# A hybrid encoder step: squares of the head norm on ScalarE, and the memory's split behind the weight casts

## The chip, the cores and the metric

One core of a Trainium2 chip runs the program: TensorE (PE) multiplies, VectorE (DVE), ScalarE (ACT) and GpSimd (POOL) compute elementwise, SyncE (SP) issues most transfers. The metric is device time of one execution in microseconds. Before the change the median of three runs is 962.3 us (962.19 to 962.57).

## The reference, cut to what matters

The step runs two layers over 256 prompt frames and 32 sample frames (T = 288 columns) with D_MODEL 1024. Layer 0 has one input projection that feeds two groups of heads: A, chunk-band attention, and B, forgetting attention. Both normalise query and key by head (64 rows):

```python
def rmsnorm(x, g):
    xf = x.astype(jnp.float32)
    y = xf * lax.rsqrt(jnp.mean(xf * xf, axis=-1, keepdims=True) + EPS)
    return (y * g.astype(jnp.float32)).astype(x.dtype)
```

Layer 1 has stick-breaking attention without that norm. After its mixer each layer attends across 256 memory tokens, whose keys and values are made from `rmsnorm(mem, g_mem) @ w_kv`, and then runs a squared-ReLU MLP of four times the width. The weights are float32 and are read once; the core reads 148.65 MB in all.

## The kernel before, in words

Activations lie transposed: 128 features on the partitions, 288 frames along the free axis, eight such tiles (`KT`). A product runs as three TensorE products on split operands (`mm3`, lines 156 to 160): high part by high part, high by low, low by high. So each weight is split on the core. `load_chunk` (118 to 145) loads 256 columns of a weight matrix in two halves of 512 KB by SP into a pool of four raw buffers (`wraw`), ACT casts the high part (`wh`, L143, in the first layer's mixer two casts of 128x512 per half), and DVE or POOL subtracts it for the low part (`wl`, L144). Three split halves fit ahead of PE. The activations are split the same way.

`headnorm` (408 to 413) sums squares over 64 partitions by a product with a block-diagonal matrix of ones. The squares too are split in a high and a low part: ACT writes `sqh` (L410), DVE casts it to `sh` (L341) and subtracts to `sl` (L343), both in `two_parts`; PE adds both products up in `ps_hn` (L348, L349); ACT takes logarithm and exponential for the root (L182, L183). It runs 16 times: four projections, query and key, two halves each. `two_parts` also serves the norms of cross attention and of the memory's keys. These tiles and others are drawn from eight scratch buffers of one tag (`f`).

`ORD_AB` (line 32) orders the steps of layer 0's mixer: `q`: query and key of a group, `p`: values, `a`: attention, `F`: the forget gate, `M`: the memory's split (`mem_split`), `N`: the memory's root mean square (`mem_rms`), `K`: the memory's keys of one head. `mem_split` loads the memory in two parts of 512 KB into the same raw buffers as the weights, and in eight steps casts it times a gain (`mh`, ACT L313), subtracts (`ml`, DVE L314), squares (ACT L317, L320) and adds the squares on DVE (L321). `mem_rms` sums over partitions on PE (L332, L335) and takes roots on ACT. In layer 1 the same function runs without the squares and sums.

A planner of the tile framework simulates the whole program with its own costs and writes the order of each engine and of SP's queue; earlier lines have priority, and a buffer is given out as it comes free in that simulation. On the chip each engine then runs its order without change and waits where something is late. `issue_after` puts all instructions of a block behind a given one on that one's engine.

Of the kernel before, what the change touches and what calls it, by code (L numbers as in the profile page):

```python
# [8 lines left out]
F32 = mybir.dt.float32  # L9
F32R = mybir.dt.float32r  # L10
AF = mybir.ActivationFunctionType
ALU = mybir.AluOpType
AX = mybir.AxisListType

P = 128
NP_ = 256
NS = 32
T = NP_ + NS
KT = 8
CW = 256  # L20
FB = 8
# [7 lines left out]
HPE = 0  # L29
HPG = 0  # L30
VT2 = 1
ORD_AB = 'qA0 pA0 F qA1 pA1 aA0 qB0 aA1 qB1 pB0 M pB1 aB0 N K2 aB1 K0 K3 K1'.split()
ORD_C = 'M q0 k0 v0 q1 k1 v1 m0 q2 k2 v2 m1 q3 k3 v3 m2 m3'.split()
FILL_C = 96, 30, 12
ORD_X = 's1 s2 s3 s0 v0 v1 S v2 v3'.split()
# [16 lines left out]
def body(ctx: ExitStack, tc: tile.TileContext, i: dict, o: dict):  # L52
    nc = tc.nc
    mm = nc.tensor.matmul
    dve = nc.vector
    act = nc.scalar.activation

    const = ctx.enter_context(tc.tile_pool(name="const", bufs=1))
    wraw = ctx.enter_context(tc.tile_pool(name="wraw", bufs=WR))
# [4 lines left out]
    scr = ctx.enter_context(tc.tile_pool(name="scr", bufs=2))  # L64
# [7 lines left out]
    class R:  # L72
        stack = None
        count = 0
        step = 4
        c = 0
        after = None
# [18 lines left out]
    def bank(pool, name):  # L96
        return pool.tile([P, 512], F32, tag="b", name=name)
# [20 lines left out]
    def load_chunk(ap, w=CW, split=2, before=None):  # L118

        nk = KT // split  # L120
        ws = []
        for s in range(split):
            raw = wraw.tile([P, nk, w], F32, tag="raw", name="raw")
            if before is None:
                nc.sync.dma_start(out=raw, in_=ap[:, s * nk:(s + 1) * nk, :])
            nq = min(nk, NQ) if split > 1 else nk
            step = min(nq, R.step) if before is None else 1
            for k in range(0, nk, step):
                if k % nq == 0:
                    wh = wspl.tile([P, nq, w], F32R, tag="wh", name="wh")  # L130
                    wl = wspl.tile([P, nq, w], F32R, tag="wl", name="wl")
                    ws += [(wh[:, j, :], wl[:, j, :]) for j in range(nq)]
                r, src = slice(k % nq, k % nq + step), raw[:, k:k + step, :]
                if before is not None:
                    nc.sync.dma_start(out=src, in_=ap[:, s * nk + k:s * nk + k + 1, :])
                    before(s * nk + k)
                R.count += 1
                e = nc.gpsimd if R.pool_every and R.count % R.pool_every == 0 and before is None else dve
                with ahead(HPS):
                    if R.dve_every and R.count % R.dve_every == 0 and before is None:  # L140
                        dve.tensor_copy(wh[:, r, :], src)  # L141
                    else:
                        act(wh[:, r, :], src, AF.Copy)  # L143
                    e.tensor_tensor(wl[:, r, :], src, wh[:, r, :].bitcast(F32), ALU.subtract)  # L144
        return ws

    def ahead(n):
        return tc.high_priority(n) if n else ExitStack()
# [32 lines left out]
    def rstd_of(ps, n, inv, out):  # L181
        act(out, ps, AF.Ln, bias=epsb, scale=inv)  # L182
        act(out, out, AF.Exp, scale=-0.5)  # L183
# [69 lines left out]
    def first(k):  # L253
        nc.scalar.dma_start(out=h[:, k, :], in_=i["xT"][:, k, :])
        n0.split(k)

    ws0 = load_chunk(i["ab_w"][0], before=first)
    xh, xl, rs = n0.rms(SQP)

# [10 lines left out]
    for a in range(4):  # L270
        r = slice(32 * a, 32 * a + 32)
# [11 lines left out]
    bdr = const.tile([P, P], F32R, name="bdr")  # L283
# [13 lines left out]
    memrs = const.tile([P, NP_], F32, name="memrs")  # L297
    memrt = const.tile([P, 2], F32, name="memrt")

    def mem_split(layer, put=None):  # L300

        mh = spp.tile([P, KT, T], F32R, tag="sp", name="mh")
        ml = spp.tile([P, KT, T], F32R, tag="sp", name="ml")
        ssum = scr.tile([P, T], F32, tag="ssum", name="mssum", bufs=2) if layer == 0 else None
        raws = []

        def step(k):
            if k % 4 == 0:
                raws.append(wraw.tile([P, 4, NP_], F32, tag="raw", name="mraw"))
                nc.sync.dma_start(out=raws[-1], in_=i["memT"][:, k:k + 4, :])  # L310
            m = raws[-1][:, k % 4, :]
            g = gT[:, 3, layer, k:k + 1]
            act(mh[:, k, 0:NP_], m, AF.Copy, scale=g)  # L313
            dve.scalar_tensor_tensor(ml[:, k, 0:NP_], m, g, mh[:, k, 0:NP_].bitcast(F32), ALU.mult, ALU.subtract)  # L314
            if layer == 0:
                if k == 0:
                    act(ssum[:, 0:NP_], m, AF.Square)  # L317
                else:
                    sq = scr.tile([P, T], F32, tag="f", bufs=FB, name="sqm")
                    act(sq[:, 0:NP_], m, AF.Square)  # L320
                    dve.tensor_tensor(ssum[:, 0:NP_], ssum[:, 0:NP_], sq[:, 0:NP_], ALU.add)  # L321

        for k in range(KT):
            if put is None:
                step(k)
            else:
                put(k, lambda k=k: step(k))
        return mh, ml, ssum

    def mem_rms(ssum):  # L330
        ps = bank(R.m, "ps_ms")
        mm(ps[:, 0:NP_], ones, ssum[:, 0:NP_], start=True, stop=True)  # L332
        rstd_of(ps[:, 0:NP_], NP_, 1.0 / 1024, memrs)
        for j in range(2):
            mm(ps[:, NP_ + j:NP_ + j + 1], ssum[:, j * P:(j + 1) * P], ones[:, 0:1], start=True, stop=True)  # L335
        rstd_of(ps[:, NP_:NP_ + 2], 2, 1.0 / 1024, memrt)

    def two_parts(sq, n):

        sh = scr.tile([P, T], F32R, tag="f", bufs=FB, name="sh")  # L340
        dve.tensor_copy(sh[:, 0:n], sq[:, 0:n])  # L341
        sl = scr.tile([P, T], F32R, tag="f", bufs=FB, name="sl")
        (nc.gpsimd if HNP else dve).tensor_tensor(sl[:, 0:n], sq[:, 0:n], sh[:, 0:n].bitcast(F32), ALU.subtract)  # L343
        return sh, sl

    def add_parts(ps, sel, parts, n):

        mm(ps[:, 0:n], sel, parts[0][:, 0:n], start=True, stop=False)  # L348
        mm(ps[:, 0:n], sel, parts[1][:, 0:n], start=False, stop=True)  # L349
# [4 lines left out]
    def xnorm_parts(t, n):  # L354
        sq = []
        for d in range(2):
            sq.append(scr.tile([P, T], F32, tag="f", bufs=FB, name="sqx"))
            act(sq[d][:, 0:n], t[:, d, 0:n], AF.Square)
        dve.tensor_tensor(sq[0][:, 0:n], sq[0][:, 0:n], sq[1][:, 0:n], ALU.add)
        return two_parts(sq[0], n)  # L360
# [9 lines left out]
    def mem_k(layer, hd, mh, ml):  # L370
        ws = load_chunk(i["w_kv"][layer, hd])
        t = scr.tile([P, 2, T], F32, tag="t2", name="tmk")
        pss = gemm2(ws, mh, ml, NP_)
        for d in range(2):
            ps = pss[d]
            dve.tensor_tensor(t[:, d, 0:NP_], ps[:, 0:NP_], memrs, ALU.mult)
        return mem_k_norm(layer, hd, t, xnorm_parts(t, NP_))
# [28 lines left out]


    def headnorm(t, r):
        sq = scr.tile([P, T], F32, tag="f", bufs=FB, name="sqh")
        act(sq, t, AF.Square)  # L410
        ps = bank(R.m, "ps_hn")
        add_parts(ps, bdr, two_parts(sq, T), T)
        rstd_of(ps[:, 0:T], T, 1.0 / 64, r)

    def project_qk(wname, cq, ck, xh, xl, rs, norm, ko, oidx, ws0=None):
# [160 lines left out]
    class Mix:  # L576
# [55 lines left out]
        def run(self, steps):  # L632
            xh, xl, rs = self.x
            for step in steps:
                op, g = step[0], int(step[1:] or 0)
                if op == "M":
                    mem = mem_split(1)[0:2]
                elif op == "q":
                    qz = R.ph.tile([P, 2, T], F32, tag="qz", name="qz", bufs=QZB[1])
# [314 lines left out]
    def project_ab(kind, g):  # L954
        return project_qk("ab_w", 6 * kind + g, 6 * kind + 2 + g, xh, xl, rs, kind, "ab"[kind] + "kT", g,
                          ws0 if kind == 0 and g == 0 else None)

    def values_ab(kind, g):
        return project_v("ab_w", 6 * kind + 4 + g, xh, xl, rs, "ab"[kind] + "vT", g)
# [30 lines left out]
    qk, vs, mk0 = {}, {}, {}  # L990
    for step in ORD_AB:
        op, at = step[0], step[1:]
        kind, g = ("AB".index(at[0]), int(at[1])) if len(at) == 2 else (0, 0)
        if op == "q":
            qk[at] = project_ab(kind, g)
        elif op == "p":
            vs[at] = values_ab(kind, g)
        elif op == "a":
            group_ab(kind, g, *qk[at], vs[at])
        elif op == "F":  # L1000
            forget()
        elif op == "M":
            mh, ml, msum = mem_split(0)
        elif op == "N":

            with tc.issue_after(last_mm[0].ins):
                mem_rms(msum)
        else:
            R.after = last_mm[0].ins if at == "0" else R.after
            mk0[int(at)] = mem_k(0, int(at), mh, ml)  # L1010
# [26 lines left out]
    mh, ml = mix.mem  # L1037
# [115 lines left out]
```

## Time and profile before

| what | value |
| --- | --- |
| median of three runs | 962.3 us |
| profiled execution, and its span | 962.2 us, 960.5 us |
| PE, DVE, ACT, POOL busy | 946.5, 686.3, 526.4, 170.9 us |
| mean granted TensorE clock | 0.995 |
| layer 0's mixer | about the first 176 us |
| memory's split | 87.8 to 139.0 us, in pieces |

A page lists busy times by engine, the chain of work that ended last, and groups of instructions by source line, with the idle time of the engine in front of them and what ended it in brackets (`<-`). Timelines give start, duration, engine, line, operation, written tile `<-` read tiles. Matmuls are pipelined, so a matmul that lasts 0.29 us starts every 0.13 us. SPq is SP's queue of transfers.

### The profile page before, as it was taken

Reading aid. Unit: us, or ns where it says so; the run is one execution under the profiler, and the core shown is the slowest. Engines: PE = TensorE matmul, PEld = TensorE weight load, DVE = VectorE, ACT = ScalarE, POOL = GpSimd, SP = SyncE. Lnnn points to the kernel's source line nnn. Section 1 sums busy time; section 2 is a strip of 40 time slices with the busy share of each in tenths; the row PEclk is TensorE's granted clock in tenths of the full one; section 3 lists DMA queues with packets and bytes.
Section 4 is the critical chain, followed back from the end, with each engine's and each line's share of the span. In section 5 each row is a group of like instructions: output and inputs, shape, how many; then the busy total and the mean of one; then the engine's idle time right before and its main releaser. Section 6 shows DMA issues by size and latency. Waiting matters only on the chain.

```text
span 960.5 us, 19226 instructions
## 1 busy us (share of the span) xinstructions
PE 946.5 (99%) x7284; PEld 917.6 (96%) x7284; DVE 686.3 (71%) x1506; ACT 526.4 (55%) x1220; POOL 170.9 (18%) x200
## 2 busy tenths in 40 slices
PE   8998999999999999999999999999999999999998
PEld 7997899999999999999999899999999999999998
DVE  8788788779678766767687567778977655555643
ACT  5666577656456644444466646554644664454531
POOL 4002200021212221222100000003444111111110
PEclk9999899999999999999999999999999999999999
DMA  8654464644555554545465444465444454545452
GB/s 266 220 156 134 134 214 141 232 161 138 172 168 170 160 174 157 175 156 174 156 214 173 151 158 141 142 217 178 139 159 140 152 178 158 172 158 175 155 175 72
DMA packets 50700, 160.01 MB, mean 167 GB/s; under 512 B 6296, under 2 KB 12968, under 8 KB 50352
## 3 DMA queue, kind: packets, MB, share of 16 engines
q1 hardware_dynamic: 46864, 148.69, 48.1%
q0 software_dynamic: 2592, 8.92, 2.4%
q10 hardware_dynamic: 1152, 1.18, 0.4%
q8 instruction: 57, 0.93, 0.4%
q14 instruction: 35, 0.29, 0.1%
HBM read 148.65 MB, written 10.12 MB: 165 GB/s over the span
## 4 chain that ended last, share of the span: by engine, by line
PE 91%; DVE 5%; DMA 1%; issue 1%; ACT 1%; SPq 0%; DVEq 0%
PE g L158 27%; PE g L160 27%; PE g L159 27%; DVE wl L144 2%; DMA mraw<-in_memT_dram 1%; PE zz L753 1%; PE zz L708 1%; PE zz L504 1%; PE s L549 1%; PE sx L158 0%; DVE spl L741 0%; PE sx L160 0%; PE pox L160 0%; DVE ml L314 0%; PE ps_px L822 0%
## 5 line engine op out<-in xcount | busy, mean ns | idle before, releaser
L143 ACT ACTIVATE wh<-raw 128x512 fp32r<-128x512 f32 (+3 forms) x541 | 269.0, 547 | 242.1 <-PE g L159 129.8
L144 DVE TENSOR_TENSOR wl<-raw,wh 128x512 fp32r<-128x512 f32 (+3 forms) x519 | 318.5, 650 | 98.5 <-ACT wh L143 92.4
L158 PE MATMUL g<-xh,wh 128*128 128x288 f32 (+1 forms) x1032 | 305.6, 300 | 1.1 <-DVE t L433 0.5
L159 PE MATMUL g<-xl,wh 128*128 128x288 f32 (+1 forms) x1032 | 304.4, 297 | 1.8 <-DVE xl L196 1.8
L160 PE MATMUL g<-xh,wl 128*128 128x288 f32 (+1 forms) x1032 | 303.4, 298 | 0.6 <-DVE wl L144 0.5
L144 POOL TENSOR_TENSOR wl<-raw,wh 128x256 fp32r<-128x256 f32 (+2 forms) x105 | 123.3, 1174 | 436.6 <-ACT wh L143 328.6
L158 PEld LDWEIGHTS g<-xh,wh 128*128 128x128 f32 (+1 forms) x1032 | 193.3, 189 | 4.1 <-DVE t L433 1.1
L159 PEld LDWEIGHTS g<-xl,wh 128*128 128x128 f32 (+1 forms) x1032 | 193.7, 188 | 3.1 <-DVE xl L196 2.6
L160 PEld LDWEIGHTS g<-xh,wl 128*128 128x128 f32 (+1 forms) x1032 | 193.6, 189 | 2.7 <-DVE wl L144 1.6
L159 PE MATMUL g<-hl,wh 128*128 128x288 f32 x512 | 150.4, 295 | 0.0
L158 PE MATMUL g<-hh,wh 128*128 128x288 f32 x512 | 149.0, 295 | 0.0
L160 PE MATMUL g<-hh,wl 128*128 128x288 f32 x512 | 148.6, 294 | 0.0
L159 PEld LDWEIGHTS g<-hl,wh 128*128 128x128 f32 x512 | 96.1, 188 | 0.0
L160 PEld LDWEIGHTS g<-hh,wl 128*128 128x128 f32 x512 | 95.7, 188 | 0.0
L158 PEld LDWEIGHTS g<-hh,wh 128*128 128x128 f32 x512 | 95.3, 188 | 0.0
L159 PE MATMUL g<-ol,wh 128*128 128x288 f32 x256 | 74.9, 295 | 0.0
L158 PE MATMUL g<-oh,wh 128*128 128x288 f32 x256 | 74.0, 296 | 0.3 <-ACT oh L525 0.3
L160 PE MATMUL g<-oh,wl 128*128 128x288 f32 x256 | 73.5, 295 | 0.0
L141 DVE CAST wh<-raw 128x256 fp32r<-128x256 f32 (+2 forms) x83 | 32.4, 391 | 39.8 <-PE g L159 20.1
L905 DVE TENSOR_TENSOR h<-h,g 128x288 f32<-128x288 f32 x64 | 28.8, 450 | 29.6 <-PE g L160 29.5
L159 PEld LDWEIGHTS g<-ol,wh 128*128 128x128 f32 x256 | 48.1, 188 | 0.0
L158 PEld LDWEIGHTS g<-oh,wh 128*128 128x128 f32 x256 | 47.5, 188 | 0.6 <-ACT oh L525 0.4
(285 smaller groups left out, 1466.4 us busy)
## 6 DMA issues: line engine op xcount, KB each, us to landing
raw<-in_w_up_dram SPq DMA_DIRECT2D x64, 512.0 KB, 3.8
raw<-in_w_down_dram SPq DMA_DIRECT2D x64, 512.0 KB, 3.8
raw<-in_w_kv_dram SPq DMA_DIRECT2D x32, 512.0 KB, 3.8
raw<-in_sb_w_dram SPq DMA_DIRECT2D x24, 512.0 KB, 4.0
raw<-in_ab_w_dram SPq DMA_DIRECT2D x22, 512.0 KB, 4.8
raw<-in_w_q_dram SPq DMA_DIRECT2D x16, 512.0 KB, 3.8
raw<-in_w_o_dram SPq DMA_DIRECT2D x16, 512.0 KB, 3.8
raw<-in_ab_wo_dram SPq DMA_DIRECT2D x8, 512.0 KB, 3.9
```

The lines of the kernel that those rows point to most:

```text
L141: dve.tensor_copy(wh[:, r, :], src)
L143: act(wh[:, r, :], src, AF.Copy)
L144: e.tensor_tensor(wl[:, r, :], src, wh[:, r, :].bitcast(F32), ALU.subtract)
L158: mm(out, lh, rh, start=first, stop=False)
L159: mm(out, lh, rl, start=False, stop=False)
L160: return mm(out, ll, rh, start=False, stop=last)
L504: out.append(mm(po[64 * par:64 * par + 64, kk * P:NP_], vt[:, kk, cols], pts[par][kk], start=kk == 0, stop=kk == 1).ins)
L549: mm(s[:, 0:NP_], q[:, P:NP_], kT[:, p, 0:NP_], start=True, stop=True)
L708: mm(block(zz, e, kk), kT[r, p, kk * P:(kk + 1) * P], qz[r, p, kk * P:NP_].rearrange("p (b c) -> p b c", c=P), start=kk == 0, stop=False, ...
L753: mm(zz[:, e, 0:384], mtrir, x[:, e, :], stop=False, **k_)
L905: dve.tensor_tensor(h[:, kt, :], h[:, kt, :], ps[:, 0:T], ALU.add)
```

## The change

In `headnorm` the first part of the squares is written by a second ACT Square of the same input, with a rounded output, instead of a DVE cast of the first; the subtraction stays on DVE. The other users of `two_parts` keep the cast. `M` moves ahead of `pB0`. In layer 0 the memory's eight steps are only noted there; the two following calls of `load_chunk` (pB0's and pB1's) each issue four of them behind their last ACT cast. Both parts of the memory are now loaded at once, ahead of the steps, in both layers. In `mem_rms` the second sums stand ahead of the first root.

```diff
-ORD_AB = 'qA0 pA0 F qA1 pA1 aA0 qB0 aA1 qB1 pB0 M pB1 aB0 N K2 aB1 K0 K3 K1'.split()
+ORD_AB = 'qA0 pA0 F qA1 pA1 aA0 qB0 aA1 qB1 M pB0 pB1 aB0 N K2 aB1 K0 K3 K1'.split()
...
+        tow = []
...
-                        act(wh[:, r, :], src, AF.Copy)
+                        cast = act(wh[:, r, :], src, AF.Copy).ins
                     e.tensor_tensor(wl[:, r, :], src, wh[:, r, :].bitcast(F32), ALU.subtract)
+        if R.tow:
+
+            now, R.tow = R.tow[0:4], R.tow[4:]
+            with tc.issue_after(cast):
+                for fn in now:
+                    fn()
         return ws
...
-    def mem_split(layer, put=None):
+    def mem_split(layer, tow=False):
...
+        for k in range(0, KT, 4):
+            raws.append(wraw.tile([P, 4, NP_], F32, tag="raw", name="mraw"))
+            nc.sync.dma_start(out=raws[-1], in_=i["memT"][:, k:k + 4, :])
 
         def step(k):
-            if k % 4 == 0:
-                raws.append(wraw.tile([P, 4, NP_], F32, tag="raw", name="mraw"))
-                nc.sync.dma_start(out=raws[-1], in_=i["memT"][:, k:k + 4, :])
-            m = raws[-1][:, k % 4, :]
+            m = raws[k // 4][:, k % 4, :]
...
-        for k in range(KT):
-            if put is None:
-                step(k)
-            else:
-                put(k, lambda k=k: step(k))
+        steps = [lambda k=k: step(k) for k in range(KT)]
+        if tow:
+            R.tow = steps
+        else:
+            for fn in steps:
+                fn()
         return mh, ml, ssum
...
     def mem_rms(ssum):
         ps = bank(R.m, "ps_ms")
         mm(ps[:, 0:NP_], ones, ssum[:, 0:NP_], start=True, stop=True)
-        rstd_of(ps[:, 0:NP_], NP_, 1.0 / 1024, memrs)
         for j in range(2):
             mm(ps[:, NP_ + j:NP_ + j + 1], ssum[:, j * P:(j + 1) * P], ones[:, 0:1], start=True, stop=True)
+        rstd_of(ps[:, 0:NP_], NP_, 1.0 / 1024, memrs)
         rstd_of(ps[:, NP_:NP_ + 2], 2, 1.0 / 1024, memrt)
...
+    def square_parts(t):
+
+        sq = scr.tile([P, T], F32, tag="f", bufs=FB, name="sqh")
+        act(sq, t, AF.Square)
+        sh = scr.tile([P, T], F32R, tag="f", bufs=FB, name="sh")
+        act(sh, t, AF.Square)
+        sl = scr.tile([P, T], F32R, tag="f", bufs=FB, name="sl")
+        dve.tensor_tensor(sl, sq, sh.bitcast(F32), ALU.subtract)
+        return sh, sl
...
     def headnorm(t, r):
-        sq = scr.tile([P, T], F32, tag="f", bufs=FB, name="sqh")
-        act(sq, t, AF.Square)
         ps = bank(R.m, "ps_hn")
-        add_parts(ps, bdr, two_parts(sq, T), T)
+        add_parts(ps, bdr, square_parts(t), T)
         rstd_of(ps[:, 0:T], T, 1.0 / 64, r)
...
-            mh, ml, msum = mem_split(0)
+            mh, ml, msum = mem_split(0, tow=True)
```

## The prediction

> **What bounds the kernel now.** I read the page first, then the time by windows, then the timelines of single engines where a window fell short.
>
> ```profile
> span 960.5 us, 19226 instructions
> ...
> PE 946.5 (99%) x7284; PEld 917.6 (96%) x7284; DVE 686.3 (71%) x1506; ACT 526.4 (55%) x1220; POOL 170.9 (18%) x200
> ...
> PE 91%; DVE 5%; DMA 1%; issue 1%; ACT 1%; SPq 0%; DVEq 0%
> ```
>
> TensorE (PE) is busy 946.5 of 960.5 us, and 91% of the chain that ended last is its own work. The change adds no matmul and removes none, so it can only gain where PE stands idle or runs at a lower clock. The first window below is an undisturbed stretch of the first layer, attention included; the second is the stretch in which the memory's split now runs.
>
> ```profile
> 48.00:76.00 28.00, 28.00 (x210) 26.90 (x209) 21.42 (x71) 18.91 (x52) 1.08 (x2) 1.00 0.54 162
> 76.00:104.00 28.00, 24.92 (x174) 20.52 (x173) 24.58 (x68) 18.23 (x53) 9.48 (x11) 0.88 0.45 144
> 104.00:108.00 4.00, 3.90 (x25) 3.04 (x25) 3.46 (x8) 1.66 (x4) 0.74 (x1) 1.00 0.00 0
> ```
>
> Columns: window, length, busy time and instructions of PE, PE's weight loads, DVE, ACT and POOL, granted clock, DMA share, GB/s. From 76 to 104 PE is idle 3.08 us, and a mean clock of 0.88 costs 0.12 x 28 = 3.4 us more: 6.4 us, with 174 matmuls against 210 in the stretch before. That is nearly all that can be won here. Windows cut at the edges of the clock's steps show where it fell:
>
> ```profile
> 81.24:84.66 3.42, 2.67 (x22) 2.43 (x20) 3.42 (x7) 0.63 (x2) 1.51 (x2) 1.00 0.20 68
> ...
> 91.48:94.90 3.42, 2.10 (x31) 1.46 (x29) 3.38 (x15) 3.42 (x11) 0.32 (x1) 1.00 0.03 9
> 94.90:101.72 6.82, 6.15 (x23) 5.27 (x24) 5.61 (x15) 3.89 (x13) 1.99 (x4) 0.50 0.85 260
> ```
>
> PE idles 1.32 us between 91.48 and 94.90 and the clock is then halved for 6.82 us; 0.75 us of idle time in 81.24 to 84.66 did not do it.
>
> **The first half of the memory's split (a wait that goes).** ACT works in order:
>
> ```profile
> 87.78 0.51 ACT L313 ACTIVATE mh<-mraw,gT 128x256 fp32r<-128x256 f32 x1 [0.97 <-DMA mraw<-in_memT_dram]
> ...
> 88.50 1.29 ACT L313 ACTIVATE mh<-mraw,gT 128x256 fp32r<-128x256 f32 x3
> 89.70 0.49 ACT L491 ACTIVATE pr<-pr,nm 128x256 f32<-128x256 f32 x1
> ...
> 93.15 2.17 ACT L143 ACTIVATE wh<-raw 128x512 fp32r<-128x512 f32 x4
> 95.23 0.29 ACT L533 ACTIVATE qs<-qz 128x128 f32<-128x128 f32 x1
> ```
>
> ```profile
> 91.41 0.29 PE L160 MATMUL g<-xh,wl 128*128 128x288 f32 x1
> 92.11 0.40 PE L348 MATMUL ps_hn<-sh,bdr 128*128 128x288 f32 x1 [0.41 <-DVE sh L341]
> ...
> 95.57 1.11 PE L538 MATMUL ss<-ck,qs 128*64 128x256 f32 x2 [1.58 <-ACT qs L533]
> ```
>
> ACT waits 0.97 us for the memory's transfer and then spends until 89.70 on it: softmax and head norm behind it start 89.70 - (87.78 - 0.97) = 2.9 us late. Afterwards ACT has no gap until qs, and PE stands 1.58 us for qs. With the memory gone from this place, ACT can't be early by all of 2.9 us: the weight casts at 93.15 overwrite buffers that PE reads until 91.70 (91.41 + 0.29). So they move by 93.15 - 91.70 = 1.45, and qs with them. Term 1: -1.45 us (bounds 0 and -1.99, both PE waits).
>
> **The clock.** The 1.45 us brings the idle time of that window from 1.32 to near zero, below the 0.75 that left the clock alone. Term 2: -3.4 us, half of 6.82 (bounds 0 and -3.4). [...]
>
> **The second half.**
>
> ```profile
> 101.45 1.71 ACT L313 ACTIVATE mh<-mraw,gT 128x256 fp32r<-128x256 f32 x4 [2.20 <-DMA mraw<-in_memT_dram]
> ...
> 102.00 3.81 DVE L314 SCALAR_TENSOR_TENSOR ml<-mraw,gT,mh 128x256 fp32r<-128x256 f32 x4 [0.81 <-ACT mh L313]
> ...
> 106.07 0.44 DVE L433 TENSOR_TENSOR t<-g,rs 128x288 f32<-128x288 f32 x1
> ```
>
> ACT waits 2.20 us, then DVE is held 3.81 us by four instructions, and t, which empties a matmul bank, comes at 106.07. PE meanwhile did 25 matmuls in 104 to 108 where an undisturbed 4 us hold 30 (210 over 28 us): 5 x 28/210 = 0.7 us, for the 2.07 us of the hold that lie behind 104. At that rate 3.81 us cost 1.3. Term 3: -1.3 us (bounds 0 and -2.5, a full stop from 104 to the matmul behind t).
>
> **ScalarE writes the first part.** Of 16 head norms each loses a DVE cast and gains a second ACT Square:
>
> ```profile
> L410 ACT ACTIVATE sqh<-t x16: 426/429/444, 21.4 to 123.0; 128x288 f32<-128x288 f32 x16
> L341 DVE CAST sh<-sqh x16: 291/302/1995, 22.4 to 123.6; 128x288 fp32r<-128x288 f32 x16
> ```
>
> In the chain of one norm a cast of 0.30 gives way to a Square of 0.43 that overlaps the one before it (three mh took 1.29, so 0.40 rather than 0.49 each): about +0.04 us, sixteen times +0.6. ACT (65% busy in the quoted 76 to 104) has room, DVE (88%) gains some. Term 4: +0.6 us (bounds -0.5 and +2). [...]
>
> One cast is worth more. POOL's additions on the decay bias hold DVE up:
>
> ```profile
> 79.60 2.09 POOL L975 TENSOR_TENSOR b<-b,cq 128x1024 f32<-128x1024 f32 x1
> ```
>
> ```profile
> 79.86 2.00 DVE L341 CAST sh<-sqh 128x288 fp32r<-128x288 f32 x1
> 84.22 0.44 DVE L343 TENSOR_TENSOR sl<-sqh,sh 128x288 fp32r<-128x288 f32 x1
> ...
> 99.95 1.23 DVE L343 TENSOR_TENSOR sl<-sqh,sh 128x288 fp32r<-128x288 f32 x1
> ```
>
> ```profile
> 84.72 0.40 PE L349 MATMUL ps_hn<-sl,bdr 128*128 128x288 f32 x1 [0.81 <-DVE sl L343]
> ```
>
> The cast begun at 79.86 ends with POOL's addition, and PE later waits 0.81 us for sl. Without the cast, sl takes that place, stretched as at 99.95 to 1.23, so DVE is ahead by 2.00 + 0.44 - 1.23 = 1.2 us, and next in line is the softmax maximum. Term 5: -1.0 us (bounds 0 and -1.6).
>
> **Where the memory's work goes.** Its two loads move ahead of pB0's two on the SP queue:
>
> ```profile
> 77.86 0.37 SPq L125 DMA_DIRECT2D raw<-in_ab_w_dram  x1
> ...
> 96.17 0.35 SPq L310 DMA_DIRECT2D mraw<-in_memT_dram  x1
> ```
>
> ```profile
> DMA to landing us min/median/max: 3.8/3.9/5.3
> ```
>
> All four share the pool of four raw buffers, so pB0's halves take the places in time that the memory had, the second 96.17 instead of 77.86 (no other queue is passed; the steps issue nothing on POOL's). It lands by 96.17 + 5.3 = 101.5, and its cast starts at 108.32 now: 6.8 us of cover, which shrinks as PE gets earlier, though the buffer is then freed earlier too. Term 6: +0.4 us (bounds 0 and +2).
>
> The eight steps now stand behind pB0's and pB1's last casts, about 109 and 120:
>
> ```profile
> 108.32 1.15 ACT L143 ACTIVATE wh<-raw 128x512 fp32r<-128x512 f32 x2 [0.62 <-PE g L159]
> ...
> 127.92 1.94 ACT L320 ACTIVATE sqm<-mraw 128x256 f32<-128x256 f32 x6
> ```
>
> ```profile
> 108.00:118.00 10.00, 9.49 (x88) 8.37 (x87) 6.63 (x16) 5.77 (x13) 0.86 (x2) 1.00 0.46 151
> 118.00:128.00 10.00, 10.00 (x79) 9.98 (x78) 7.30 (x16) 6.38 (x16) 0.54 (x1) 1.00 0.43 149
> ```
>
> Four steps cost ACT 1.71 for the casts and 4 x 0.32 (six squares in 1.94) for squares: 3.0 us. DVE pays four steps at 0.48 and up to four additions at 0.42 (minimum, median, maximum in ns below):
>
> ```profile
> L314 DVE SCALAR_TENSOR_TENSOR ml<-mraw,gT,mh x16: 471/482/1826, 88.3 to 487.5; 128x256 fp32r<-128x256 f32 x16
> ...
> L321 DVE TENSOR_TENSOR mssum<-mssum,sqm x7: 416/419/421, 128.7 to 139.0; 128x256 f32<-128x256 f32 x7
> ```
>
> That is 3.6 us less about four casts saved, 1.2. ACT is idle 4.2 and 3.6 us in the two windows, DVE 3.4 and 2.7: both halves fit, tightly. Queued behind them are the head norms of the last query/key group and pB1's transposed values, on which PE waits. I take half of one block, term 7: +1.5 us (bounds 0 and +6.0, two blocks wholly in PE's way; without the idle time as cover they cost that). The memory's products follow on PE some 4 us behind the second half, so nothing waits for mh:
>
> ```profile
> 127.86 0.28 PE L158 MATMUL g<-mh,wh 128*128 128x256 f32 x1
> ```
>
> **Sums ahead of roots.**
>
> ```profile
> 140.18 0.60 PE L332 MATMUL ps_ms<-mssum,ones 128*128 128x256 f32 x2
> ...
> 141.34 0.61 PE L335 MATMUL ps_ms<-ones,mssum 128*128 128x1 f32 x4
> ```
>
> The second sums wait until ACT's first root has read the bank: 141.34 - 140.78 = 0.56 us, into which PE can put attention work. Nearer to nothing, then. Term 8: -0.2 us (bounds 0 and -0.6).
>
> **Sum.** -1.45 - 3.4 - 1.3 + 0.6 - 1.0 + 0.4 + 1.5 - 0.2 = -4.85. The profiled execution took 962.2 us (span 960.5 and 1.7 around it), 0.1 under the median of 962.3. So 957.4 us.
>
> **The rivals.**
> (A) The half clock stays or moves. The planner orders every engine anew from its own cost model; qs keeps four weight casts in front of it, and a gap of 1 us elsewhere in a thin window does the same. For it: 81.24 to 84.66 already holds 0.75 us of idle time. Against: term 1 closes the one window that fell, and term 5 thins the other. Without term 2: 962.3 - 1.45 = 960.9.
> (B) Slower: the towed blocks. At 109 and 120 ACT and DVE are given 3 us each in one piece; if the planner lets them go ahead of t and r of the last head norms, PE idles up to term 7's bound, and a new gap over 1.32 us in one window halves the clock for 6.8 us. Then +6.0 + 3.4 in place of +1.5: -4.85 + 7.9 = +3.05, 965.3 us. It decides once the new stalls exceed 6.4 us together. For it: DVE would be at 9 of 10 us from 108 on (6.63 + 2.4). Against: PE has weight products to do there, and the blocks wait for no transfer.
> (C) Nothing moves, because the squares can't come early: they need scratch tiles (eight for all norms) which the last head norms hold; the six of 127.92 stand there now though their data was there by 101.45. So the memory's raw buffers stay taken and later loads start late, while the freed time is eaten by the next wait. Terms 1, 3 and 5 halve, the clock term goes, 6 and 7 stay: -1.9 + 2.3 = 962.7.
> (D) More than forecast: blocks and transfers wholly hidden (terms 4, 6, 7 at zero): -7.35, 955.0.
>
> **How the numbers follow.** Forecast 0.42 (own range 955.5 to 960.0), A 0.18, B 0.18, C 0.10, D 0.12. About 0.2%, 1.9 us, is what a measurement tells from no change. Faster: forecast, D, and 0.10 of A, 0.64. Same: 0.08 of A, C's 0.10, 0.18. Slower: B, 0.18. The range 953 to 964.5 takes in D with the clock and other terms near their good bounds, A and C, and B's milder half.
>
> **What would show it.** Step 1: no wait of ACT's mh on the memory's transfer in the first layer, and PE's wait on qs gone or under 0.5 us. Step 2: granted clock 1.00 from 80 to 130. Step 3: no stretched ml beside POOL's additions. Steps 4, 5: no DVE cast under head norm, sh on ACT, ps_hn's wait on sl gone near 84. Step 7: mh behind wh in two groups of four, with PE idle under 1.5 us after each. Wrong it would be if PE showed a new gap behind a towed block, if half clock appeared again, or if wh casts waited on late weights.

## The result, and the profile after

The changed kernel takes 956.46 us (median of four runs, 955.00 to 957.54), the kernel before 962.3 us (962.19 to 962.57). The ratio is 0.9938, with a 95% interval of 0.9921 to 0.9955: 5.8 us faster. Run again later beside other variants it took 954.92 us (five runs, 954.72 to 956.86) against 961.97, a ratio of 0.9933 (0.9921 to 0.9945). The profiled execution of the first set took 956.56 us. Two executions that lie far off the others of their kernel are left out of the medians below: 1296.26 us of the move without the tow, and 3206.80 us of the changed kernel without POOL's additions, the only one of that kernel that was profiled.

The page of the changed kernel: span, busy times, the chain that ended last.

```profile
span 954.8 us, 19232 instructions
...
PE 943.2 (99%) x7284; PEld 917.8 (96%) x7284; DVE 682.9 (72%) x1490; ACT 530.7 (56%) x1236; POOL 171.8 (18%) x200
...
PE 94%; DVE 4%; ACT 1%; issue 1%; DMA 0%; SPq 0%; DVEq 0%; ACTq 0%
```

DVE lost sixteen instructions and ACT gained sixteen, one for each head norm. The same stretches as before, by windows (length, busy time and count of PE, its weight loads, DVE, ACT, POOL, then granted clock, DMA share, GB/s):

```profile
48.00:76.00 28.00, 28.00 (x213) 27.27 (x211) 22.07 (x69) 21.33 (x60) 1.38 (x3) 1.00 0.57 173
76.00:104.00 28.00, 28.00 (x227) 25.09 (x227) 24.23 (x69) 21.10 (x60) 9.97 (x10) 1.00 0.51 161
104.00:108.00 4.00, 2.17 (x17) 1.94 (x16) 4.00 (x8) 1.73 (x5) 1.90 (x2) 1.00 0.39 122
108.00:118.00 10.00, 10.00 (x68) 9.37 (x67) 7.23 (x16) 7.26 (x18) 0.56 (x1) 0.83 0.30 101
```

The bad stretch, 76 to 104, is whole: PE has no idle time, the clock is 1.00, and it does 227 matmuls where it did 174. But a hole that was not there stands at 104 to 108: 2.17 us busy of 4.00, and behind it the clock is halved again (0.50 from 108.22 to 111.63). In the single timelines of PE, DVE and POOL it looks like this (start, duration, engine, line, operation, written tile `<-` read tiles, idle time before):

```profile
107.14 0.40 PE L165 MATMUL g<-xh,wh 128*128 128x288 f32 x1 [1.83 <-DVE vT L481]
```

```profile
97.44 1.29 DVE L145 TENSOR_TENSOR wl<-raw,wh 128x512 fp32r<-128x512 f32 x2 [1.44 <-ACT wh L144]
98.65 1.70 DVE L321 SCALAR_TENSOR_TENSOR ml<-mraw,gT,mh 128x256 fp32r<-128x256 f32 x4
100.91 0.80 DVE L361 TENSOR_TENSOR sl<-sqh,sh 128x288 fp32r<-128x288 f32 x1 [0.57 <-ACT sh L359]
101.64 3.42 DVE L145 TENSOR_TENSOR wl<-raw,wh 128x512 fp32r<-128x512 f32 x2
104.98 0.41 DVE L537 TENSOR_TENSOR ol<-po,oh 128x256 fp32r<-128x256 f32 x1
105.31 1.40 DVE L454 SCALAR_TENSOR_TENSOR qz<-t,qg,r 128x288 f32<-128x288 f32 x2
106.64 0.44 DVE L481 TENSOR_TENSOR vT<-g,rs 128x288 f32<-128x288 f32 x1
```

```profile
102.18 2.32 POOL L991 TENSOR_TENSOR b<-b,cq 128x1024 f32<-128x1024 f32 x1
```

Two weight subtractions that take 1.29 us at 97.44 take 3.42 at 101.64, beside POOL's addition on the decay bias. The two qz behind them take 1.40 us, where the next two (107.37) take 0.93. vT, which empties a matmul bank, comes behind all of these, and PE stands 1.83 us. The four ml at 98.65 are the first towed block.

How much of the gain is where: the memory's first products start at 121.8 instead of 127.9, and the last ones of layer 1 at 623.2 instead of 628.8. Before first, after second:

```profile
L158 PE MATMUL g<-mh,wh x128: 274/281/387, 127.9 to 628.8; 128*128 128x256 f32 x128
```

```profile
L165 PE MATMUL g<-mh,wh x128: 274/282/387, 121.8 to 623.2; 128*128 128x256 f32 x128
```

The span shortened by 5.7 us (960.5 to 954.8) and the last of these products moved by 5.6: nothing is won later. It is there by the end of layer 0's mixer, whose output projection comes at 171.01 instead of 176.66:

```profile
176.66 0.66 PE L158 MATMUL g<-oh,wh 128*128 128x288 f32 x3 [0.31 <-ACT oh L525]
```

```profile
171.01 0.67 PE L165 MATMUL g<-oh,wh 128*128 128x288 f32 x3 [0.32 <-ACT oh L541]
```

### The profile page after: what moved, and what is told of

The parts are those of the page before. It is cut to its first block, busy times and chain, and to the rows that moved or that the text cites. A ratio compares the mean times of both kernels' runs of the same rounds, so it can differ in the third digit from the quotient of the medians.

```text
span 954.8 us, 19232 instructions
## 1 busy us (share of the span) xinstructions
PE 943.2 (99%) x7284; PEld 917.8 (96%) x7284; DVE 682.9 (72%) x1490; ACT 530.7 (56%) x1236; POOL 171.8 (18%) x200
## 4 chain that ended last, share of the span: by engine, by line
PE 94%; DVE 4%; ACT 1%; issue 1%; DMA 0%; SPq 0%; DVEq 0%; ACTq 0%
PE g L165 28%; PE g L167 27%; PE g L166 27%; DVE wl L145 2%; PE zz L769 1%; PE s L565 1%; PE zz L724 1%; PE po L520 1%; PE zz L520 1%; DMA raw<-in_ab_w_dram 0%; DVE spl L757 0%; PE sx L165 0%; PE sx L167 0%; PE pox L167 0%; PE ps_px L838 0%
## 5 line engine op out<-in xcount | busy, mean ns | idle before, releaser
L145 DVE TENSOR_TENSOR wl<-raw,wh 128x512 fp32r<-128x512 f32 (+3 forms) x519 | 323.0, 659 | 99.7 <-ACT wh L144 93.7
```

## The experiments

The experiments ran in three sets, each in five rounds beside the kernel before on one chip: 961.70 us in the first set and 961.78 in the second, on the same chip, and 961.97 in the third, on another.

### One part at a time

Theory M is the prediction's own sum: the memory's split is what is worth moving, the squares nearly nothing. Rival S: the squares carry it. Four kernels each hold one part of the change. In the first only `headnorm` is edited:

```diff
     def headnorm(t, r):
-        sq = scr.tile([P, T], F32, tag="f", bufs=FB, name="sqh")
-        act(sq, t, AF.Square)
         ps = bank(R.m, "ps_hn")
-        add_parts(ps, bdr, two_parts(sq, T), T)
+        add_parts(ps, bdr, square_parts(t), T)
```

> The kernel before, with ScalarE writing the first part of the head norm's squares and nothing else. Theory M (the gain is the memory's place: its wait on ScalarE and the half clock behind it): terms 4 and 5 of the prediction, +0.6 - 1.0 = -0.4 us, so about 961.9, and PE still waits over 1 us for qs near 95 with a clock of 0.5 behind it. Rival S (the gain is the cast taken off VectorE, which was held by GpSimd's additions): at least half of the 5.8 us, 959.4 or less, with PE's waits on sl and sh gone.

Measured: 954.08 us (953.01 to 954.36), ratio 0.9920 (0.9906 to 0.9933), a gain of 7.6 us, as rival S had it. By the medians that is the whole effect of the change and more (the intervals overlap), from the part that the sum had at a loss of 0.6, with 1.0 for one cast.

The second holds the memory part without the squares: `M` moved, both loads at once, steps towed (two lines of the edit).

```diff
-... qB1 pB0 M pB1 aB0 ...
+... qB1 M pB0 pB1 aB0 ...
-            mh, ml, msum = mem_split(0)
+            mh, ml, msum = mem_split(0, tow=True)
```

> The memory's part alone: M ahead of pB0, both loads at once, steps towed behind the casts; the cast on VectorE and the order of sums and roots are those of before. Theory M: terms 1, 2, 3, 6 and 7, -1.45 - 3.4 - 1.3 + 0.4 + 1.5 = -4.25, so about 958.0, no wait of mh for its transfer. Rival S: 960.5 or more.

Measured: 955.50 us (955.35 to 955.76), ratio 0.9936 (0.9923 to 0.9948), a gain of 6.2 us, more than either theory had for it. The third is the second with the steps left to the planner:

```diff
-            mh, ml, msum = mem_split(0, tow=True)
+            mh, ml, msum = mem_split(0)
```

> The memory moved ahead of pB0 with both loads at once, but its steps not towed: they follow as the planner likes, ahead of pB0's casts. If the wait for the transfer was the cost (theory M), the earlier load takes it away and the time is within 1.5 us of the memory's part alone, about 958. If the place of the work on ScalarE and VectorE is the cost (rival W), the steps stay in the crowded stretch from 80 to 104 and it takes 960.5 to 963.

Measured: 960.75 us (959.92 to 962.55), ratio 0.9991 (0.9982 to 1.0000): about 0.9 us, in the range of rival W. So of the memory part neither the place of `M` nor the early load gains; the queueing behind the casts does. The fourth has the sums ahead of the roots alone:

```diff
-        rstd_of(ps[:, 0:NP_], NP_, 1.0 / 1024, memrs)
         for j in range(2):
             mm(ps[:, NP_ + j:NP_ + j + 1], ssum[:, j * P:(j + 1) * P], ones[:, 0:1], start=True, stop=True)
+        rstd_of(ps[:, 0:NP_], NP_, 1.0 / 1024, memrs)
```

> The kernel before with the memory's sums ahead of its roots and nothing else. Term 8: -0.2 us, bounds 0 and -0.6, so 961.7 to 962.3: no difference that can be told. A rival that has the planner draw a new order from any edit gives more than 1 us either way.

Measured: 961.74 us, ratio 1.0000 (0.9991 to 1.0009): nothing.

The windows show what the first two have in common. First the squares alone, then the memory part, then the memory part without the tow:

```profile
76.00:104.00 28.00, 27.79 (x229) 25.06 (x226) 26.10 (x75) 22.36 (x64) 9.02 (x10) 1.00 0.51 167
104.00:108.00 4.00, 3.91 (x30) 3.53 (x31) 2.36 (x6) 3.06 (x8) 2.27 (x2) 1.00 0.11 42
```

```profile
76.00:104.00 28.00, 27.18 (x213) 23.08 (x212) 24.36 (x69) 18.55 (x54) 10.92 (x12) 1.00 0.43 146
104.00:108.00 4.00, 3.28 (x24) 3.22 (x24) 4.00 (x10) 2.91 (x8) 0.00 (x0) 1.00 0.41 135
```

```profile
76.00:104.00 28.00, 25.25 (x182) 20.79 (x181) 21.97 (x72) 18.59 (x55) 6.41 (x9) 0.94 0.40 134
```

Either part by itself fills the stretch in which PE stood, so they can't add: 7.6 + 6.2 + 0 = 13.8 us alone, 5.8 to 7.1 together. With the squares alone the memory's first cast still waits for its transfer and still stands in the crowded stretch (mh at 83.04), and it costs PE next to nothing:

```profile
83.04 0.51 ACT L319 ACTIVATE mh<-mraw,gT 128x256 fp32r<-128x256 f32 x1 [0.27 <-DMA mraw<-in_memT_dram]
```

### Why the squares are worth so much

One head norm before and after, ACT's and DVE's part. Before:

```profile
76.80 0.43 ACT L410 ACTIVATE sqh<-t 128x288 f32<-128x288 f32 x1
```

```profile
77.91 2.03 DVE L438 SCALAR_TENSOR_TENSOR qz<-t,qg,r 128x288 f32<-128x288 f32 x2
...
81.84 2.13 DVE L144 TENSOR_TENSOR wl<-raw,wh 128x512 fp32r<-128x512 f32 x2
```

The cast of this square is the one quoted at 79.86 (2.00 us), its subtraction the one at 84.22: sl ends 7.86 us after sqh began. The same norm after:

```profile
74.87 0.43 ACT L357 ACTIVATE sqh<-t 128x288 f32<-128x288 f32 x1
75.20 0.43 ACT L359 ACTIVATE sh<-t 128x288 fp32r<-128x288 f32 x1
```

```profile
75.67 0.46 DVE L361 TENSOR_TENSOR sl<-sqh,sh 128x288 fp32r<-128x288 f32 x1 [0.15 <-ACT sh L359]
```

75.67 + 0.46 - 74.87 = 1.26 us. Summed over the sixteen norms, the time from sqh's start to sl's end falls from 37.8 to 26.9 us; 6.6 of these 11 us lie in this one norm. Before, the square went through DVE's queue twice, as a cast and as a subtraction. In this norm the cast stood behind two qz and was itself stretched beside POOL's addition, and the subtraction stood behind two weight subtractions (the rows above). Now the square passes there once.

Three things changed together, though: the second pass, DVE's load, and with the load the casts that POOL held. Theory L says the load and the stretching by POOL count, theory Q that the pass and the order of the engines behind it do. The first test takes POOL's additions out of the kernel before. They add a number that is constant along each row of a softmax, so without them the softmax is the same.

```diff
-                cqj = cq[:, j, 4 * g:4 * g + 4].unsqueeze(2).to_broadcast([P, 4, n])
-                nc.gpsimd.tensor_tensor(d, b1[:, :, 0:n], cqj, ALU.add)
-                nc.gpsimd.affine_select(d, d, pattern=[[0, 4], [-1, n]], ...
+                nc.gpsimd.affine_select(d, b1[:, :, 0:n], pattern=[[0, 4], [-1, n]], ...
```

> The kernel before without GpSimd's additions of the query's decay to the bias of forgetting attention (a constant per row, which the softmax cancels); GpSimd's masking stays. Theory L (VectorE's instructions held by those additions, 77.9 to 84.0, start the stall, and the cast is only the worst hit): the stall from 84 to 104 and its half clock go without any part of the change, 956.5 or less. Rival Q (two passes of each head norm through VectorE's queue are the cause, whatever GpSimd does): gains under 2 us, 960 or more.

Measured: 958.87 us (956.98 to 959.71), ratio 0.9964 (0.9950 to 0.9978): 2.9 us, between the two. The stretched cast is gone, its maximum 310 ns instead of 1995, and still the norm quoted above takes 5.06 us from sqh's start to sl's end (7.86 before, 1.26 with the change):

```profile
L341 DVE CAST sh<-sqh x16: 292/303/310, 22.5 to 120.5; 128x288 fp32r<-128x288 f32 x16
```

The wait for qs is still there, and so is lost clock:

```profile
93.73 0.65 PE L538 MATMUL ss<-ck,qs 128*64 128x256 f32 x2 [1.59 <-ACT qs L533]
```

```profile
76.00:104.00 28.00, 25.74 (x190) 21.44 (x189) 21.75 (x72) 19.04 (x56) 4.06 (x7) 0.94 0.41 136
```

The second test is the squares alone, with DVE's load put back: a cast into a tile that nobody reads.

```diff
         act(sh, t, AF.Square)
+        jc = R.ph.tile([P, T], F32R, tag="jc", bufs=1, name="jc")
+        dve.tensor_copy(jc, sq)
```

> Squares on ScalarE alone, and VectorE still makes the cast, into a tile that nobody reads: VectorE's load is that of before, but the norm's chain passes its queue once. Theory Q (the second pass through the queue): within 1.5 us of the squares alone, 954 to 955.6. Theory V (VectorE's load, the cast held by GpSimd included): the stall comes back, 959 to 962.

Measured: 956.93 us (956.55 to 957.24), ratio 0.9949 (0.9936 to 0.9962): 4.85 of the 7.6 us remain, 2.8 go with the cast. That lies between the two forecasts, nearer to Q's. The cast that was put back meets none of POOL's additions (its longest is 311 ns), so this kernel tests VectorE's load without the stretch. In its profile PE is held at a new place, for 2.29 us, and the clock falls behind it (a mean of 0.65 from 104 to 108):

```profile
104.11 0.40 PE L165 MATMUL g<-xh,wh 128*128 128x288 f32 x1 [2.29 <-DVE t L450]
```

So with DVE's instruction count as before, taking the cast off the norm's path still gives about two thirds; the rest goes with DVE's time. The planner orders the engines anew in each of these kernels, so the split holds for these programs and isn't a price of the two causes by themselves.

Two more kernels leave POOL's additions out of the changed kernel and of the squares alone (the same edit).

> The changed kernel without the same additions. Theory L: its one large stall, 1.83 us of PE at 105.3 behind a low weight part that VectorE takes 3.42 us for beside GpSimd's addition at 102.18, and the 3.4 us of half clock behind it (1.7 us), go: 956.5 - 3.5 = 953. Rival Q: 956 to 957, the stall is ScalarE's towed block ahead of it at 97.83 and stays.

> Squares on ScalarE alone (954.1), again without GpSimd's additions. Theory L: the two remedies close the same stall, so little is added, 952.5 to 954. Rival Q: independent gains, the same difference as between the kernel before and the kernel before without additions.

Measured: 954.05 us, ratio 0.9918 (0.9904 to 0.9932), and 953.15 us, ratio 0.9911 (0.9897 to 0.9925), the lowest ratio of all, 8.6 us under the kernel before. Both intervals overlap those of the kernels they were made from (0.9921 to 0.9955 and 0.9906 to 0.9933), so the additions' price, 2.9 us before, isn't resolved once the squares are on ACT; both times lie nearer to theory L's. Whether the hole of the changed kernel closed without them, no trace shows.

### What the memory part costs beside the squares

By the medians the changed kernel gains less than the squares alone (5.8 and 7.1 us against 7.6), though the intervals overlap. Theory T: the towed block brings the two weight subtractions beside POOL's addition. Theory P: any edit beside the squares gets a new order from the planner and loses part of the gain. The changed kernel itself first, for comparison on one chip:

> The changed kernel itself, so that the parts can be compared with it on one chip. 956.5 us by every theory, with PE idle about 1.8 us near 105, behind the two weight subtractions on DVE that stand beside POOL's addition. Theory T (the towed block is what brings those two to that place) and theory P (every engine is ordered anew by the planner, and any edit beside the squares alone, which took 954.1, loses a part of the gain) differ in the next two kernels.

Measured: 954.92 us, with the same hole, PE idle for 1.91 us at 107.00. Then the changed kernel with `M` at its old place, still towed:

```diff
-... qB1 M pB0 pB1 aB0 ...
+... qB1 pB0 M pB1 aB0 ...
```

Here the second half of the steps goes behind the weight load after `N`, so the memory's sums are taken over the first half of its features alone (PE's sums at 121, DVE's last addition at 131.5); all steps still run. So its trace tells where the pair falls, but its time isn't that of a kernel that waits for all of the sums.

> The changed kernel with M behind pB0 as before, still towed and loaded at once: the blocks go behind the casts of pB1 and of the load after it, about 10 us later. Theory T: the two subtractions no longer stand behind a block ahead of 102, no stall near 105, 954.1 us as with the squares alone. Theory P: a stall of 1 to 2 us at another place, 956 to 957 us.

Measured: 953.61 us (953.56 to 953.63), ratio 0.9913 (0.9900 to 0.9926), and no hole. DVE and POOL at the place:

```profile
98.82 0.46 DVE L361 TENSOR_TENSOR sl<-sqh,sh 128x288 fp32r<-128x288 f32 x1 [0.28 <-ACT sh L359]
99.20 0.94 DVE L454 SCALAR_TENSOR_TENSOR qz<-t,qg,r 128x288 f32<-128x288 f32 x2
100.06 2.57 DVE L145 TENSOR_TENSOR wl<-raw,wh 128x512 fp32r<-128x512 f32 x2
102.55 0.41 DVE L537 TENSOR_TENSOR ol<-po,oh 128x256 fp32r<-128x256 f32 x1
102.88 0.44 DVE L449 TENSOR_TENSOR t<-g,rs 128x288 f32<-128x288 f32 x1
```

```profile
102.06 2.32 POOL L991 TENSOR_TENSOR b<-b,cq 128x1024 f32<-128x1024 f32 x1
```

Without the block ahead of it the pair starts at 100.06 instead of 101.64. It is stretched here too, to 2.57 us, beside POOL's short addition (100.00 to 101.04), but it is nearly done when the long one begins at 102.06, and t comes at 102.88. PE has no wait there:

```profile
104.00:108.00 4.00, 4.00 (x33) 3.83 (x32) 3.21 (x6) 2.72 (x7) 1.60 (x2) 1.00 0.35 117
```

The third keeps the new place and takes the tow away:

```diff
-            mh, ml, msum = mem_split(0, tow=True)
+            mh, ml, msum = mem_split(0)
```

> The changed kernel with M at its new place and loaded at once, but its steps not towed: they follow the planner's priority at that place. Theory T: no block behind the casts, no stall near 105, 954 to 955 us. Theory P: with the memory part alone the tow was worth 5.3 us (960.8 against 955.5), mostly by stalls of 1.8 us near 88 and 1.3 us near 110; if these come with the squares too, 957 to 959 us.

Measured: 959.64 us (954.96 to 960.96), ratio 0.9963 (0.9946 to 0.9981). Theory T had no hole here, and it fell on that point: the hole is larger, and the time lies above theory P's range too. Its runs also lie far apart: 954.96 us at a mean clock of 1.000, 955.65 and 958.55 at 0.996, and four from 959.64 to 960.96 at 0.993 and 0.994. The profiled one is of the last kind (959.77; half clock again, a mean of 0.87 from 104 to 108 and of 0.88 from 108 to 118), so whether the hole stands in the quickest run no trace shows.

```profile
100.86 4.60 DVE L145 TENSOR_TENSOR wl<-raw,wh 128x512 fp32r<-128x512 f32 x2 [0.30 <-ACT wh L144]
```

```profile
106.21 0.40 PE L165 MATMUL g<-xh,wh 128*128 128x288 f32 x1 [3.51 <-DVE t L449]
```

`M` now stands ahead of `pB0` in the order, so without the tow its steps have priority over pB0's casts, and ACT runs the other seven of the memory's casts in a row (next row, 2.90 us) in the middle of the attention. The pair of subtractions meets both of POOL's additions (from 100.84 and 103.00; 4.60 us). What holds in all three traces is the second half of T: whether the pair falls beside POOL's long addition. The tow is one way to bring it there, the lack of one another.

```profile
81.06 2.90 ACT L320 ACTIVATE mh<-mraw,gT 128x256 fp32r<-128x256 f32 x7
```

Last, the changed kernel with the root ahead of the sums as before:

```diff
+        rstd_of(ps[:, 0:NP_], NP_, 1.0 / 1024, memrs)
         for j in range(2):
             mm(ps[:, NP_ + j:NP_ + j + 1], ssum[:, j * P:(j + 1) * P], ones[:, 0:1], start=True, stop=True)
-        rstd_of(ps[:, 0:NP_], NP_, 1.0 / 1024, memrs)
```

> The changed kernel with the root ahead of the second sums, as before. Alone the sums' order gave nothing (961.7 against 961.7). If the edits of this part act by their own cost, 956.5 us here too; if the planner's order of the rest hangs on it, it differs by a microsecond or more, and the stall near 105 is gone or moved.

Measured: 954.77 us (954.41 to 956.30), ratio 0.9927 (0.9915 to 0.9939). The same as the changed kernel beside it, hole included (2.1 us at 107.24).

## Why the prediction was right, and where its steps were not

The total was forecast at 957.4 us and measured at 956.46 and 954.92. It came out that near by luck: wrong terms made up for each other.

**What bounds the kernel.** Right. Nearly all that was won lay in 76 to 104, and what follows the mixer moved as a whole.

**The first half of the memory's split (-1.45) and the second (-1.3).** What they described is gone: after the change PE has no wait on qs, mh waits for no transfer in layer 0, and the longest ml is 610 ns instead of 1826.

```profile
L321 DVE SCALAR_TENSOR_TENSOR ml<-mraw,gT,mh x16: 472/480/610, 98.6 to 481.8; 128x256 fp32r<-128x256 f32 x16
```

The cause was incomplete. The memory part alone is worth 6.2 us and not what these two and the clock come to net of the costs; with the same early loads and no tow it is worth 0.9. It isn't the transfer's wait that counted but the place of the work on ACT and DVE.

**The clock (-3.4).** This step failed: a mean clock of 0.88 was read as 3.4 us to be won. Half clock did come again, in the profiled run behind the new hole, which the prediction had named as showing it wrong: 3.41 us there and 6.83 at the start, the same 10.2 in all as before. And over the runs of the kernel before the clock does not set the time. Times (mean clock) of the third set:

```
before       961.62 (0.998)  961.92 (0.998)  961.97 (0.998)  962.25 (0.998)
             961.29 (0.995)  961.64 (0.996)  961.96 (0.996)  961.96 (0.996)
             962.07 (0.995)  962.18 (0.995)  962.22 (0.997)  962.44 (0.995)
the changed  954.72 (0.998)  954.90 (0.998)  954.92 (0.998)  956.40 (0.994)  956.86 (0.994)
```

Before, the mean is 961.94 at 0.998 and 961.93 at 0.996 and below, though 0.003 of 960 us is 2.9 us of full clock. The profiled run of the sums alone shows in part why. Its engines have the order of the kernel before as far as 112 us, and half clock lasts 3.41 us there (97.36 to 100.77) instead of 6.82, which is worth 1.7 us of full clock. But PE then waits at two places where the kernel before has no wait, and the wait for t that ended at 112.30 (first row below) ends only 0.59 us earlier, of which 0.24 were there before the half clock (qs, 95.33 against 95.57):

```profile
112.30 0.40 PE L158 MATMUL g<-xh,wh 128*128 128x288 f32 x1 [0.51 <-DVE t L433]
```

```profile
97.00 0.40 PE L165 MATMUL g<-xh,wh 128*128 128x288 f32 x1 [0.54 <-DVE t L450]
105.97 0.40 PE L165 MATMUL g<-xh,wh 128*128 128x288 f32 x1 [0.22 <-DVE t L450]
111.71 0.40 PE L165 MATMUL g<-xh,wh 128*128 128x288 f32 x1 [0.51 <-DVE t L450]
```

What PE did late at half clock, it mostly would have waited for at full. This holds for the kernel before as it is: without POOL's additions its two runs at clock 1.000 took 956.98 and 957.90 us, the three at 0.994 and 0.995 took 958.87 to 959.71.

**ScalarE writes the first part (+0.6, and -1.0 for one cast).** This is the mis-sized term: -7.6 us measured alone. The step "in the chain of one norm a cast of 0.30 gives way to a Square of 0.43" priced the instructions by their durations. The rows it quoted for one norm also showed the rest: the subtraction started 4.36 us after the cast (84.22 against 79.86), only 2.00 of them the cast's own, and the cast itself came 3.06 us after its square (76.80, quoted above). In that norm a pass through the crowded queue cost what stood in front, not the instruction's own time. The Square's 0.43 was right (430 ns), and it lay beside other work.

**Transfers and buffers (+0.4).** From 76 to 130 no weight cast waits for a transfer after the change, and the waits of ACT on DMA there are gone. Nothing was to be paid.

**The towed blocks (+1.5).** Right in size and partly in kind. The tow puts a block of four ahead of DVE's next work, and PE stands 1.83 us, over the 1.5 us that the prediction allowed. The place was wrong: the blocks came behind the casts at 96.77 and 109.31, not at 109 and 120, because the whole stretch had moved up, and only the first hurt. And the block itself fits; it hurts by pushing two subtractions into POOL's addition. Against the squares alone it is 0.8 us (954.92 against 954.08, not on one chip), and 1.3 against the variant without the hole, whose sums don't wait for the second block.

**Sums ahead of roots (-0.2).** Nothing, alone and taken out.

**The rivals.** A's half clock came, and its time, 960.9, did not, since the squares gained far more than A's sum had for them. B's new gap came in small. C was right that the memory's squares can't come early (120.04, though both loads were issued by 76), and wrong that it costs: a weight load did wait for them (the one at 124.11 starts as the last square ends, at 124.08), but no cast of 76 to 130 waited for a transfer.

```profile
120.04 1.64 ACT L327 ACTIVATE sqm<-mraw 128x256 f32<-128x256 f32 x5
```

D's 955.0 is what the kernel shows in the runs at clock 0.998, on other grounds. None of the rivals had the squares as the main gain.

## What to carry to other kernels

Price an instruction on a crowded engine by how often its result passes through that engine's queue and what stands ahead there each time, not by its duration; here one cast of 0.3 us less per norm on VectorE's queue was worth 7.6 us over sixteen norms, and one norm in the crowded stretch was shortened by 6.6. Edits that relieve the same crowded stretch do not add, so try each alone: here the squares alone (954.08 us) needed none of the rest. Half clock cost nothing that could be measured in the kernel before (961.94 us at a mean clock of 0.998, 961.93 at 0.996 and below), where other engines held TensorE, and its full half behind the hole of the changed kernel (1.7 us of 3.41), where TensorE set the time; so compare runs of one kernel at different clocks before counting on it.

## What the runs showed of the hardware

The same hole halves the clock in one run and not in another. The profiled runs of the changed kernel, first the one of 956.56 us, then the one of 954.90:

```profile
104.80:108.22 3.42, 1.59 (x13) 1.36 (x12) 3.42 (x8) 1.95 (x5) 1.18 (x1) 1.00 0.48 153
108.22:111.63 3.41, 3.41 (x16) 3.13 (x17) 2.19 (x6) 2.67 (x8) 0.00 (x0) 0.50 0.00 0
```

```profile
104.80:108.22 3.42, 1.51 (x12) 1.28 (x11) 3.42 (x9) 2.01 (x6) 1.04 (x1) 1.00 0.45 153
108.22:111.63 3.41, 3.41 (x29) 2.93 (x29) 2.60 (x6) 3.16 (x8) 0.00 (x0) 1.00 0.00 0
```

PE is idle for 1.83 and 1.91 us; then it does 16 matmuls in 3.41 us in the one and 29 in the other. 13 matmuls at 0.13 us are 1.7 us, and that is also how the times of this kernel part: 954.72 to 955.00 at clock 0.998, 956.37 to 957.54 at 0.994 to 0.996. Here PE sets the time, and the half clock is paid in full. So 1.83 us of idle time was followed by half clock, for 3.41 us, and 1.91 us at the same place was not: the prediction's yardstick, 1.32 us of idle time against 0.75, doesn't tell the two apart. What decides between them, no run shows.

Beside POOL's additions two pieces of DVE's work lasted until shortly behind an addition's end: the cast took 1995 ns instead of 302 and ended at 81.86, the addition at 81.69; the pair of weight subtractions took 3.42 us instead of 1.29, which is 2.13 more beside an addition of 2.32, and ended at 105.06, the addition at 104.50. Those 0.56 us came again in the other two traces where the pair met the long addition: 0.55 in the second run of the changed kernel, 0.56 without the tow. Without the additions no cast of a head norm's square is over 310 ns. How an addition holds VectorE, no row shows.
